# Two small matmul blocks of a gated DeltaNet kernel placed 22 matmuls behind their transpositions, one pacing rule for all pairs of heads, and a gate tile moved forward

## The chip, the cores and the metric

The kernel runs on one core of a Trainium2 chip. A core has a matrix engine, TensorE (PE in the profile; its weight loads have a row of their own, PEld), a vector engine (VectorE, DVE), a scalar engine for activations and copies (ScalarE, ACT), a general engine (GpSimd, POOL) and SyncE (SP), which here starts the large loads. The engines run side by side and wait for each other through semaphores. The metric is the time on the device in microseconds: 2536.32 us is the median of three runs of the kernel before (2536.3, 2536.32 and 2543.08). The profile comes from a further, separate execution.

## The reference

One layer of a streaming encoder over 512 positions of width 2048. All of it is in float32. Its parts:

```
proj = rmsnorm(x, g_pre) @ w_in                 # 145 column tiles of 128
q, k, v = silu(causal_conv4(qkv))               # 16 heads of 128
A = (k*beta) @ k.T * decay * strict             # per chunk of 64 positions
T = triangular_solve(I + A, I)                  # unit lower triangular
for chunk in 8: v_new, o, S = delta rule with T, decay and the running state S
o_a = rmsnorm(o, g_dn_out) * silu(z_a);  y_a = o_a @ w_br_a
u = silu(layernorm(causal_conv31(glu) + b_dw)) * silu(z_b);  y_b = u @ w_br_b
mixed = (sigmoid(gate_a)*y_a + sigmoid(gate_b)*y_b) @ w_out
x = x + rmsnorm(mixed, g_post)
x = x + rmsnorm(sigmoid(x @ w_ple_gate) * (p @ w_ple_proj), g_ple)
```

The change touches the third and fourth lines, where each pair of heads inverts its triangular blocks, and the place of one of the 16 tiles of gate_a.

## The kernel before

**The tile stream.** All large products run through `gemm_cm` (L169): a tile is one column block of 128 outputs by 512 positions, and takes 16 steps of the inner dimension. Every float32 operand is split in a high and a low part, so a step is three matmuls of 128x512 (L182, L184, L186; `g` is the accumulator): 48 for a tile. Jobs are queued in `jobs`, and `run_jobs` (L158) runs them in order. The weights come by SyncE into `raw`, are rounded by ScalarE (L127, the high part of `w`), and VectorE takes the rest (L128, the low part). When a tile is done, `evac` reads its accumulator. For a tile of q, k or v that is `conv4` (L405): one ScalarE operation (L408) and three VectorE operations (L410) on `cv`. For a gate tile it is one sigmoid on ScalarE (L716). There are two accumulators, so a tile's accumulator must be read before the next tile but one starts.

**What runs beside the stream.** The work for a pair of heads is a Python generator, `group(g)`, g from 0 to 7, spawned after the six q, k and v tiles of its pair. `tick()` (L142) is called after each of the 48 matmuls of a tile: it counts down every spawned generator and lets it emit its next instructions when its count is out. `yield n` asks for n matmuls of the stream before the next instructions, and a bare `yield` for HP = 4. So a number behind a yield is a distance on TensorE's queue, measured in matmuls of the stream. The layer that records the program keeps this order nearly as it is, and moves an instruction by a few places where its own estimate says that its input comes late. TensorE executes its matmuls in order: one whose input isn't there holds all behind it.

**Inside a group.** After transpositions and a 64x64 product for each chunk, VectorE inverts the 32x32 blocks by back substitution: 31 steps, each a product (L604, into `prod`) and a sum (L605, into `VT`). After each step the generator yields in proportion to the step's size times `pace`, 2.6 for the groups 0 to 6 and 1.85 for group 7 (L597). Then:

- VectorE transposes `VT` into `Vd` (L612); after one bare yield, for each of the four quadrants of 32 partitions, ScalarE copies `Vd` into `VP` (L618) and VectorE transposes that into `Tc` (L619).
- `yield 10`.
- TensorE computes `py` (L625, 16 products of 32x32; each reads the left half of `Tc`, which the quadrants 0 and 2 write) and `pz` (L628, 16 products of 64x64; each reads both halves of `Tc`). In the trace each float32 product of this kind is two matmuls, so 32 and 32.
- ScalarE copies `py` to `Y` (L632) and `pz` to `VP` (L635); 14 matmuls of the stream later TensorE computes `pd` (L640), from which ScalarE (L644) and VectorE (L646) complete `VP`.
- Ten matmuls later the scan over eight chunks starts, for both heads at once (`head_scan`, L446): in each chunk `psB` (L468), ScalarE's `vz` (L471), `psS` (L474), VectorE's new state `S` (L479), `psA` (L462), VectorE's `Xz` (L464), 14 matmuls of the stream for each chunk. It ends with `po` (L503, into the pool `wps` of two buffers), which VectorE reads (L511) into the head's output `oa`. The first product of the next group, `pk` (L532), takes a buffer of the same pool.

A group is spawned every eight tiles (six of q, k, v and two of z), so every 384 matmuls. Behind the last pair's two z tiles the queue holds three tiles of gate_a and the two tiles of the first GLU pair (L723 to L726). Then `finish("heads")` emits what is left of the last group without any stream beside it, and the buffers of the heads are given back. The next stage (L754 to L764) alternates tiles of `w_br_a`, the remaining gates and the GLU pairs, each of which spawns a convolution of 31 taps on VectorE.

Of the kernel before, what the change touches and what calls it, by code (L numbers as in the profile page):

```python
# [19 lines left out]
NK = D // P  # L20
NH = 16
# [61 lines left out]
def _body(ctx, tc, A, out):  # L83
# [82 lines left out]
    def w_in_tile(t):  # L166
        return A["w_in"][t]

    def gemm_cm(src, rhs, evac):  # L169
        if src is not None:  # L170
            prep_src.extend([src[0], src[1]])

        def job():
            ps = gps.tile([P, T], F32, tag="g", name="g")
            for qt in range(4):
                hi, lo = next_piece()
                for kk in range(4):
                    k = qt * 4 + kk
                    rh, rl = rhs[k]
                    wh = hi[:, kk * P:(kk + 1) * P]  # L180
                    wl = lo[:, kk * P:(kk + 1) * P]
                    mm(ps, wh, rh, start=(k == 0), stop=False)  # L182
                    tick()
                    mm(ps, wh, rl, start=False, stop=False)  # L184
                    tick()
                    mm(ps, wl, rh, start=False, stop=(k == NK - 1))  # L186
                    tick()
            evac(ps)
        jobs.append(job)
# [324 lines left out]
    def group(g):  # L514
# [79 lines left out]
        nc.vector.memset(UTf[:, 0:1024:33], 1.0)  # L594
        yield
        prod = hd.tile([P, 256], F32, tag="prod", name="prod", bufs=1)
        owed, pace = 0.0, 2.6 if g < NH // 2 - 1 else 1.85  # L597
        for j in range(30, -1, -1):
            n, i0 = 32 - j, j // 4
            ni = 8 - i0  # L600
# [10 lines left out]
        Vd = hd.tile([P, 8, 4, 8], F32, tag="Vd", name="Vd", bufs=1)  # L611
        nc.vector.transpose(Vd.rearrange("p i r x -> p (i r x)"), VT.rearrange("p j i -> p i j"))  # L612
        yield
        for qd in range(4):
            r = slice(32 * qd, 32 * qd + 32)
            b, par = 32 * (qd % 2), qd // 2
            dst = VP[r, :, par, b:b + 32]
            nc.scalar.copy(dst.rearrange("p x (i r) -> p x i r", r=4), Vd[r].rearrange("p i r x -> p x i r"))  # L618
            nc.vector.transpose(Tc[r, :, b:b + 32], dst)  # L619
        yield 10  # L620
        pz = wps.tile([P, 8, 64], F32, tag="w", name="pz")
        py = wps.tile([P, 8, 32], F32, tag="w", name="py")
        for x in range(8):
# [35 lines left out]
    for g in range(NH // 2):  # L659
        pair = (2 * g, 2 * g + 1)  # L660
        for h in pair:
            gemm_cm(w_in_tile(16 + h), hT, evac_k(h))
            gemm_cm(w_in_tile(h), hT, evac_q(h))
            gemm_cm(w_in_tile(32 + h), hT, evac_v(h))
        jobs.append(lambda g=g: spawn(group(g), HP, "heads"))
        for h in pair:
            gemm_cm(w_in_tile(Z_TILE0 + h), hT, evac_z(h))
# [38 lines left out]
    def glu_pair(i):  # L706
        gemm_cm(w_in_tile(GLU_TILE0 + 16 + i), hT, evac_glu_b(i))
        gemm_cm(w_in_tile(GLU_TILE0 + i), hT, evac_glu_a(i))
# [4 lines left out]
    def evac_gate(dst, i, col):  # L713
        def f(ps):
            gt = slots.tile([P, T], F32, tag="s", name="gt")
            nc.scalar.activation(gt, ps, AF.Sigmoid, bias=vv(V_BG + col))  # L716
            dst[i] = gt
        return f

    def gate_a(i):  # L720
        gemm_cm(w_in_tile(GATE_TILE0 + i), hT, evac_gate(mixed, i, i))

    for i in range(3):  # L723
        gate_a(i)
    glu_pair(0)
    run_jobs()  # L726
# [22 lines left out]
    def evac_ya(i):  # L749
        def f(ps):  # L750
            nc.vector.tensor_tensor(mixed[i], ps, mixed[i], ALU.mult)
        return f

    gate_a(3)  # L754
    glu_pair(1)
    jobs.append(lambda: finish("oa"))
    nglu = 2
    for i in range(NK):
        gemm_cm(A["w_br_a"][i], oT, evac_ya(i))
        if i + 4 < NK:  # L760
            gate_a(i + 4)
        if nglu < NK:
            glu_pair(nglu)
            nglu += 1  # L764
# [594 lines left out]
```

## Time and profile before

| | |
|---|---|
| median of three runs | 2536.32 us |
| the profiled execution, on the device | 2543.33 us |
| its span in the profile | 2541.6 us |
| mean granted TensorE clock | 0.991 |
| VectorE busy | 1652.4 us (65%) |
| ScalarE busy | 1054.8 us (42%) |
| DMA, mean rate | 110 GB/s |

The span is the time from the first to the last recorded instruction; the device time is 1.7 us longer. Busy time is what an engine spent in instructions, and idle time in front of an instruction is put down to whatever the instruction waited for last. The profile models the end of a matmul, and consecutive ones overlap: a 128x512 matmul is listed with 0.39 us, while the starts of two in a row lie 0.23 us apart, and it is the distance of the starts that says how fast the stream goes. "Granted clock" is the share of TensorE's full clock that it was given in a stretch. A timeline lists the start in us, the duration in us, the engine, the source line, the operation, the written and read tiles and their sizes, how often, and in brackets the idle time before it and what ended it.

### The profile page before, as it was taken

The page shows a single profiled execution, that of the slowest core. Times are in us where ns is not written, and L with a number is a line of the kernel's source. Part 1 is how long each engine was busy: PE and PEld are TensorE (multiplying, and loading weights), DVE is VectorE, ACT ScalarE, POOL GpSimd, SP SyncE. Part 2 cuts the span into 40 slices and gives each one's busy share as a digit, 9 for nine tenths or more (in the row PEclk, how much of TensorE's full clock was granted, in tenths as well). Part 3 has the DMA queues.
Part 4 walks back from the last instruction along what each step waited for, and adds up shares of the span by engine and source line. Part 5 has one row for each costly group of instructions (what it writes and reads, how often), then busy time and mean ns, then how long its engine had stood idle before and what let it go on. Part 6 is the DMA issues. An engine that isn't in the chain of part 4 may idle for free.

```text
span 2541.6 us, 32595 instructions
## 1 busy us (share of the span) xinstructions
PE 2490.6 (98%) x12202; PEld 2052.7 (81%) x12202; DVE 1652.4 (65%) x3092; ACT 1054.8 (42%) x2083; POOL 135.6 (5%) x151
## 2 busy tenths in 40 slices
PE   9999999999999999999999999999999999999998
PEld 7878787887878878888888888887888888787787
DVE  6766767767676775977786868947423334776744
ACT  6655454555545455322222222235422223544532
POOL 0100000000000000000000000002000000010000
PEclk9999999999999999999999999999999999999999
DMA  6322222222222222333333332432333223676552
GB/s 256 121 87 71 84 71 84 80 75 88 71 84 71 83 75 67 108 102 102 104 100 104 104 108 96 141 129 94 98 100 99 92 100 100 179 217 217 191 174 75
DMA packets 85406, 279.45 MB, mean 110 GB/s; under 512 B 9472, under 2 KB 9728, under 8 KB 85248
## 3 DMA queue, kind: packets, MB, share of 16 engines
q1 hardware_dynamic: 81792, 266.89, 31.5%
q0 software_dynamic: 2304, 8.39, 1.9%
q10 hardware_dynamic: 1152, 2.10, 0.3%
q8 instruction: 95, 1.56, 0.2%
q14 instruction: 63, 0.52, 0.1%
HBM read 262.66 MB, written 14.68 MB: 109 GB/s over the span
## 4 chain that ended last, share of the span: by engine, by line
PE 83%; DVE 11%; issue 2%; DMA 2%; ACT 1%; POOL 0%; SPq 0%; DVEq 0%; POOLq 0%; ACTq 0%
PE g L184 22%; PE g L186 22%; PE g L182 22%; DVE prod L604 3%; DVE VT L605 2%; DVE w L128 2%; PE f L1213 2%; DMA raw<-in_w_out 2%; PE f L1214 2%; PE f L1212 2%; PE psB L468 1%; PE f L1057 1%; PE psS L474 1%; DVE cv L410 1%; PE psA L462 1%
## 5 line engine op out<-in xcount | busy, mean ns | idle before, releaser
L186 PE MATMUL g<-hh,w 128*128 128x512 f32 x2320 | 921.0, 397 | 1.6 <-DVE w L128 1.6
L184 PE MATMUL g<-hl,w 128*128 128x512 f32 x2320 | 919.1, 396 | 0.0
L182 PE MATMUL g<-hh,w 128*128 128x512 f32 x2320 | 913.0, 394 | 0.0
L128 DVE TENSOR_TENSOR w<-raw,w 128x512 fp32r<-128x512 f32 x780 | 551.9, 711 | 479.8 <-ACT w L127 477.2
L127 ACT CAST w<-raw 128x512 fp32r<-128x512 f32 x780 | 479.1, 619 | 917.3 <-PE g L186 802.3
L186 PEld LDWEIGHTS g<-hh,w 128*128 128x128 f32 x2320 | 438.5, 189 | 88.8 <-DVE w L128 4.7
L184 PEld LDWEIGHTS g<-hl,w 128*128 128x128 f32 x2320 | 438.1, 189 | 88.7 <-issue 1.6
L182 PEld LDWEIGHTS g<-hh,w 128*128 128x128 f32 x2320 | 438.4, 189 | 85.4 <-issue 0.2
L689 DVE SCALAR_TENSOR_TENSOR uc<-sg,vec,uc 128x483 f32<-128x483 f32 (+14 forms) x480 | 351.8, 734 | 14.0 <-ACT uc L686 4.0
L410 DVE SCALAR_TENSOR_TENSOR cv<-g,vec,cv 128x511 f32<-128x511 f32 x144 | 106.2, 738 | 29.8 <-ACT cv L408 29.5
L182 PE MATMUL g<-oh,w 128*128 128x512 f32 x256 | 99.6, 389 | 0.0
L184 PE MATMUL g<-ol,w 128*128 128x512 f32 x256 | 99.6, 389 | 0.0
L186 PE MATMUL g<-oh,w 128*128 128x512 f32 x256 | 99.6, 389 | 0.0
L182 PE MATMUL g<-uh,w 128*128 128x512 f32 x256 | 99.6, 389 | 0.0
L184 PE MATMUL g<-ul,w 128*128 128x512 f32 x256 | 99.6, 389 | 0.0
L186 PE MATMUL g<-uh,w 128*128 128x512 f32 x256 | 99.6, 389 | 0.0
L604 DVE TENSOR_TENSOR prod<-UT,VT 128x2 f32<-128x2 f32 (+30 forms) x248 | 87.2, 352 | 6.7
L1057 PE MATMUL f<-wsp,oph 128*128 128x512 f32 x192 | 76.5, 399 | 4.4 <-DVE wsp L1033 4.4
L1056 PE MATMUL f<-wsp,oph 128*128 128x512 f32 x192 | 75.0, 398 | 2.8 <-ACT wsp L1032 2.8
L1213 PE MATMUL f<-w,xh 128*128 128x512 f32 x192 | 75.0, 391 | 1.9 <-DVE w L128 1.9
L1058 PE MATMUL f<-wsp,opl 128*128 128x512 f32 x192 | 75.4, 393 | 0.0
L1212 PE MATMUL f<-w,xh 128*128 128x512 f32 x192 | 75.1, 392 | 0.0
(298 smaller groups left out, 2685.8 us busy)
## 6 DMA issues: line engine op xcount, KB each, us to landing
raw<-in_w_in SPq DMA_DIRECT2D x290, 512.0 KB, 3.3
raw<-in_w_ple_gate SPq DMA_DIRECT2D x40, 512.0 KB, 3.4
raw<-in_w_out SPq DMA_DIRECT2D x35, 512.0 KB, 5.1
raw<-in_w_br_a SPq DMA_DIRECT2D x32, 512.0 KB, 3.3
raw<-in_w_br_b SPq DMA_DIRECT2D x32, 512.0 KB, 3.3
t<-in_w_out POOLq DMA_DIRECT2D x16, 512.0 KB, 7.4
rw<-in_w_out SPq DMA_DIRECT2D x9, 512.0 KB, 4.4
x<-in_x SPq DMA_DIRECT2D x8, 512.0 KB, 9.4
```

Of the source, the lines that this page charges most:

```text
L127: nc.scalar.copy(hi, rq)
L128: nc.vector.tensor_tensor(lo, rq, hi.bitcast(F32), ALU.subtract)
L182: mm(ps, wh, rh, start=(k == 0), stop=False)
L184: mm(ps, wh, rl, start=False, stop=False)
L186: mm(ps, wl, rh, start=False, stop=(k == NK - 1))
L410: nc.vector.scalar_tensor_tensor(y[:, s:], ps[:, 0:T - s], vv(w0 + 3 - s), y[:, s:], ALU.mult, ALU.add)
L604: pin(nc.vector.tensor_tensor(pv_, um, vm, ALU.mult))
L689: nc.vector.scalar_tensor_tensor(y[:, s:], u[:, 0:T - s], vv(w0 + TAPS - 1 - s), y[:, s:], ALU.mult, ALU.add)
L1057: mm(ps, lh, wl[:, c], start=False, stop=False)
L1058: mm(ps, ll, wh[:, c], start=False, stop=kk == 7)
L1212: mm(ps[tt], lh, wh, start=k == 0, stop=False)
L1213: mm(ps[tt], lh, wl, start=False, stop=False)
```

## The change

Four edits. The back substitution of the last pair is paced like the others (2.6). The four quadrants are copied and transposed in the order 0, 2, 1, 3. The distance between the transpositions and `py` and `pz` is 22 matmuls of the stream where it was 10. Four tiles of gate_a stand in front of the first GLU pair where three stood, the next stage begins with gate tile 4, and its loop adds gate tile i + 5. The number of tiles and of every kind of instruction stays the same.

```
-        owed, pace = 0.0, 2.6 if g < NH // 2 - 1 else 1.85
+        owed, pace = 0.0, 2.6
...
-        for qd in range(4):
+        for qd in (0, 2, 1, 3):
             r = slice(32 * qd, 32 * qd + 32)
             b, par = 32 * (qd % 2), qd // 2
             dst = VP[r, :, par, b:b + 32]
             nc.scalar.copy(dst.rearrange("p x (i r) -> p x i r", r=4), Vd[r].rearrange("p i r x -> p x i r"))
             nc.vector.transpose(Tc[r, :, b:b + 32], dst)
-        yield 10
+        yield 22
         pz = wps.tile([P, 8, 64], F32, tag="w", name="pz")
         py = wps.tile([P, 8, 32], F32, tag="w", name="py")
...
-    for i in range(3):
+    for i in range(4):
         gate_a(i)
     glu_pair(0)
...
-    gate_a(3)
+    gate_a(4)
     glu_pair(1)
...
-        if i + 4 < NK:
-            gate_a(i + 4)
+        if i + 5 < NK:
+            gate_a(i + 5)
```

What this does to the order of the instructions shows at three places. Counted in matmuls of the stream from its first tile, `py` of the group 0 stood behind 554 of them and now stands behind 566; `pd` moves from 568 to 580, the first `psB` from 578 to 591, and `po` from 704 to 716, while `pk` of the group 1 stays at 724. The same holds for the groups 1 to 6, each 384 later. In the group 7 `py` moves from 3200 to 3254 and `po` from 3350 to 3404; the stage's last tile ends at 3360 before and at 3408 now.

The first place is VectorE's queue in the group 0, from the transpositions into `Tc` to the first state `S`. Before:

```order
L619 STREAM_TRANSPOSE Tc<-VP 32x8x32 x3
L128 TENSOR_TENSOR w<-raw,w 128x512 x3
L646 TENSOR_TENSOR VP<-VP,pd 32x8x32 x2
L410 SCALAR_TENSOR_TENSOR cv<-g,vec,cv 128x511
L128 TENSOR_TENSOR w<-raw,w 128x512
L410 SCALAR_TENSOR_TENSOR cv<-g,vec,cv 128x510
L477 COPY S<-psS 128x128
```

And now:

```order
L619 STREAM_TRANSPOSE Tc<-VP 32x8x32 x3
L128 TENSOR_TENSOR w<-raw,w 128x512 x3
L410 SCALAR_TENSOR_TENSOR cv<-g,vec,cv 128x511
L128 TENSOR_TENSOR w<-raw,w 128x512
L410 SCALAR_TENSOR_TENSOR cv<-g,vec,cv 128x510
L646 TENSOR_TENSOR VP<-VP,pd 32x8x32
L410 SCALAR_TENSOR_TENSOR cv<-g,vec,cv 128x509
L646 TENSOR_TENSOR VP<-VP,pd 32x8x32
L128 TENSOR_TENSOR w<-raw,w 128x512
L477 COPY S<-psS 128x128 x2
```

The two additions that complete `VP` (L646), on which the first `psB` waits, stood ahead of the three convolution operations of the tile that ends at matmul 576; now they stand among them, since `pd` comes four matmuls after that tile's end and not eight before it.

The second place is ScalarE's queue at the same point, from the copy of `pz` on. Before:

```order
L635 COPY VP<-pz 64x8x64 x2
L127 CAST w<-raw 128x512
L644 COPY VP<-pd 32x8x32 x2
L408 ACTIVATE cv<-g,vec 128x512
L127 CAST w<-raw 128x512
```

And now:

```order
L635 COPY VP<-pz 64x8x64 x2
L408 ACTIVATE cv<-g,vec 128x512
L127 CAST w<-raw 128x512
L644 COPY VP<-pd 32x8x32 x2
L127 CAST w<-raw 128x512
```

The copies of `pd` (L644) changed places with the convolution's first operation (L408).

The third place is TensorE's queue in the group 7, around its `py` and `pz`. Before:

```order
L184 MATMUL g<-hl,w 128x512
L625 MATMUL py<-Tc,W 32x32
L186 MATMUL g<-hh,w 128x512
L182 MATMUL g<-hh,w 128x512
L628 MATMUL pz<-W,Tc 64x64
L184 MATMUL g<-hl,w 128x512
L625 MATMUL py<-Tc,W 32x32 x15
L628 MATMUL pz<-W,Tc 64x64 x15
L186 MATMUL g<-hh,w 128x512
```

And now:

```order
L184 MATMUL g<-hl,w 128x512
L625 MATMUL py<-Tc,W 32x32 x16
L628 MATMUL pz<-W,Tc 64x64 x16
L186 MATMUL g<-hh,w 128x512
L182 MATMUL g<-hh,w 128x512
```

The two blocks, which the recording layer had spread over four matmuls of the stream, now stand in one piece, as they do in the other groups before and after.

## The prediction, as it was recorded before the changed kernel was run

> **What bounds the kernel now.** I read the engines' shares first, then TensorE's waits, then the clock by group of heads, then the timeline at the waits.
>
> ```profile
> PE 2490.6 (98%) x12202; PEld 2052.7 (81%) x12202; DVE 1652.4 (65%) x3092; ACT 1054.8 (42%) x2083; POOL 135.6 (5%) x151
> ```
>
> ```profile
> PE py L625 <- DVE Tc L619: 21.4, 15, 6.4
> ...
> PE f L1213 <- DVE w L128: 1.9, 1, 1.9
> ...
> PE pv L556 <- ACT junk L552: 0.3, 1, 0.3
> ```
>
> TensorE is busy for 98% of the span, so only its waits and its slow stretches can be won. The list of its waits (total us, times, longest) is led by `py`, 21.4 us in 15 waits, all for the transpositions into `Tc`; the longest, 6.4 us, stands alone. The last row ends the list: nothing in the scan costs TensorE a wait of note.
>
> The second loss is no wait. Stretches from one group's first `py` to the next one's, each 384 matmuls of the stream (groups 0 to 3, and 5), with TensorE's busy time, the granted clock, and the share and rate of DMA:
>
> ```profile
> 178.00:290.92 112.92, 110.75 (x635) 0.97 0.23 78
> 290.92:403.74 112.82, 110.64 (x635) 0.97 0.24 78
> 403.74:516.45 112.71, 110.53 (x635) 0.97 0.24 78
> 516.45:626.40 109.95, 107.77 (x636) 1.00 0.25 80
> 736.26:847.72 111.46, 109.29 (x635) 0.98 0.24 78
> ```
>
> The same work takes 109.95 us at full clock (row four) and up to 112.9 us where the clock fell. In steps of half a microsecond the first fall and its end, and the second fall, read:
>
> ```profile
> 179.00:179.50 0.50, 0.03 (x2) 1.00 1.01 410
> 179.50:180.00 0.50, 0.50 (x22) 0.57 0.07 25
> 186.00:186.50 0.50, 0.50 (x3) 0.60 0.00 0
> 186.50:187.00 0.50, 0.50 (x4) 1.00 0.00 0
> 292.00:292.50 0.50, 0.14 (x5) 0.71 0.63 254
> ```
>
> The clock halves at about 179.57 (0.57 is 0.07 us at full and 0.43 us at half clock), while TensorE waits for `py`, and returns at about 186.4. It falls again at about 292.21.
>
> **The change, part by part.** *Groups 0 to 6, the wait.* Group 3, undisturbed by the clock:
>
> ```profile
> 515.17 0.39 PE L184 MATMUL g<-hl,w 128*128 128x512 f32 x1
> 515.88 0.42 DVE L619 STREAM_TRANSPOSE Tc<-VP 32x256 f32<-32x256 f32 x1
> 516.45 0.22 PE L625 MATMUL py<-Tc,W 32*32 32x32 f32 x2 [0.88 <-DVE Tc L619]
> 516.96 1.37 DVE L619 STREAM_TRANSPOSE Tc<-VP 32x256 f32<-32x256 f32 x3
> 517.92 0.69 PE L625 MATMUL py<-Tc,W 32*32 32x32 f32 x30 [1.26 <-DVE Tc L619]
> 518.53 1.15 PE L628 MATMUL pz<-W,Tc 64*64 64x64 f32 x32
> 519.61 0.50 PE L186 MATMUL g<-hh,w 128*128 128x512 f32 x1
> 519.95 0.39 PE L182 MATMUL g<-hh,w 128*128 128x512 f32 x1
> 520.18 0.40 PE L184 MATMUL g<-hl,w 128*128 128x512 f32 x1
> ```
>
> From the stream's last matmul ahead of the blocks to the first behind them pass 519.61 - 515.17 = 4.44 us. Without a wait it would be one step of the stream (0.23, the distance of the last two rows), 32 `py` at the pace of the 30 (0.61 / 30 x 32 = 0.65) and `pz` to the next matmul (519.61 - 518.53 = 1.08): 1.96, say 2.05 with a switch. So 2.4 us are there to be won, and the question is whether 22 matmuls win them all. Twelve steps more of 0.228 move the start of `py` from 515.40 to 518.13. By the trace the quadrants are transposed from 515.88 and from 516.96 on, three in 1.37 us; in the new order 2 is second, so `py` has its input at about 517.4, 0.7 us early. `pz` would start 0.65 us later, at 518.78, and the last quadrant ends at 518.33: 0.45 us of slack. VectorE's queue ahead of the transpositions stays as it was, and TensorE doesn't wait in that stretch now, so they aren't later. **7 x 2.4 = 16.8 us.** The order of quadrants alone costs nothing, the same eight instructions being issued.
>
> *The clock.* Above 109.95 us lie 2.97, 2.87, 2.76 and 1.51 us: **10.1 us**. The low stretch shrinks from 4.4 to 2.0 us of small matmuls without a pause; in group 3 the small matmuls and even the pauses went by at full clock (its row reads 1.00), so a fall needs a longer low stretch than the small matmuls alone make, and I take all of this as gone. The two falls lie 292.21 - 179.57 = 112.64 us apart.
>
> [...]
>
> *Group 7.* Its timeline, and then VectorE's costliest groups of instructions from 914 us to the first transposition into `Tc`:
>
> ```profile
> 946.83 0.39 PE L184 MATMUL g<-hl,w 128*128 128x512 f32 x1
> 953.61 0.28 PE L625 MATMUL py<-Tc,W 32*32 32x32 f32 x2 [6.39 <-DVE Tc L619]
> 960.85 0.57 PE L182 MATMUL g<-hh,w 128*128 128x512 f32 x1
> 961.26 0.39 PE L184 MATMUL g<-hl,w 128*128 128x512 f32 x1
> ```
>
> ```profile
> L604 DVE TENSOR_TENSOR prod<-UT,VT 128x2 f32<-128x2 f32 (+30 forms) x31 | 10.8, 350 | 0.9
> L128 DVE TENSOR_TENSOR w<-raw,w 128x512 fp32r<-128x512 f32 x12 | 8.1, 680 | 0.9 <-ACT w L127 0.9
> L605 DVE TENSOR_REDUCE VT<-prod 128x1 f32<-128x2 f32 (+30 forms) x31 | 7.9, 254 | 0.9
> ```
>
> From 946.83 to 961.26, when the stream is at full pace again, pass 14.43 us with nine steps of the stream in them (one at 946.83, eight from 953.82 to 960.85) and the two blocks. At full clock that is 9 x 0.228 + 1.73 + 0.1 = 3.9 us: **10.5 us** to be won. The three rows of the second view, the costliest groups on VectorE, are its work there: 10.8 + 7.9 + 8.1 = 26.8 us. The yields of the 31 steps add up to 56.4 x pace: 104 matmuls or 23.8 us at 1.85, which VectorE can't keep, and 147 or 33.4 us at 2.6, where it has some 27 us to do. So `Tc` is early then. The group needs 54 matmuls more of the stream; the gate tile moved in front is 48 of them, and `po` at 3404 still lies ahead of 3408.
>
> *The moved gate tiles.* The same number of tiles, loads and sigmoids; each convolution up to the 13th starts one tile later, the last three where they were. Covered as long as VectorE keeps up there; if the 13th and 14th, now three tiles apart like those behind them, held up `w`, the nearest row is the longest wait for `w` in the list of waits, 1.9 us, once. I take nothing.
>
> *What comes later on.* `pd`, the scan and `po` now meet the tiles' convolutions 12 matmuls further on. Now, in group 0:
>
> ```profile
> 189.12 0.41 DVE L646 TENSOR_TENSOR VP<-VP,pd 32x256 f32<-32x256 f32 x1 [0.98 <-ACT VP L644]
> 189.97 0.42 DVE L646 TENSOR_TENSOR VP<-VP,pd 32x256 f32<-32x256 f32 x1 [0.43 <-ACT VP L644]
> 190.76 0.69 ACT L408 ACTIVATE cv<-g,vec 128x512 f32<-128x512 f32 x1 [0.83 <-PE g L186]
> 191.03 0.61 PE L468 MATMUL psB<-Xz,VP 128*128 128x128 f32 x4
> 191.49 0.75 DVE L410 SCALAR_TENSOR_TENSOR cv<-g,vec,cv 128x511 f32<-128x511 f32 x1 [1.10 <-ACT cv L408]
> 192.15 0.68 DVE L128 TENSOR_TENSOR w<-raw,w 128x512 fp32r<-128x512 f32 x1
> 192.75 0.74 DVE L410 SCALAR_TENSOR_TENSOR cv<-g,vec,cv 128x510 f32<-128x510 f32 x1
> 193.61 0.74 DVE L410 SCALAR_TENSOR_TENSOR cv<-g,vec,cv 128x509 f32<-128x509 f32 x1
> ```
>
> The tile ends at about 190.7. In the new order the second L646 follows the third L410: 0.8 (to the first) + 0.7 + 0.6 + 0.7 for the three, 0.4, 0.7, 0.4 = 4.3 us behind the tile's end, and the first `psB` waits on it. It comes 15 steps and `pd` behind the tile's end, and `pd` is 32 small matmuls, at the pace of `pz` 1.1 us: 15 x 0.228 + 1.1 = 4.5 us. That is level. Bounds: a gain is excluded, as there is no such wait to lose; the other end is the whole of the three L410, 2.2 us a group. I take 0.2 us, near the sum: **1.4 us lost** in seven groups. `pk` follows `po` at 8 matmuls where it was 20, and needs a buffer that VectorE reads `po` from: 8 x 0.228 = 1.8 us are left as cover, and what is lost if they don't do stands with the third rival.
>
> Sum: 16.8 + 10.1 + 10.5 - 1.4 = 36.0. The span goes from 2541.6 to 2505.6, and with the 1.7 us around it (2543.33 - 2541.6) the execution from 2543.3 to **2507 us**. The profiled execution lies 7.0 us above the median of 2536.32. If it had more clock falls than the runs at 2536.3, those vanish with the rest and 2507 stands; if the 7 us lie elsewhere, a run without them gives 2500. I stay with 2507 and let the range reach below 2500.
>
> **The rivals.** *The waits go, the clock falls stay* (small matmuls alone pull the clock down): 2507 + 10.1 = 2517. For it: the clock is down while `py` and `pz` run. Against it: group 3, where both ran at full clock.
>
> *The transpositions are later than 22 matmuls, so the change doesn't do what it says.* With 0.45 us of slack, one more cast between the quadrants (0.68) leaves 0.2 us a group; if half the present wait stayed, 7 x 1.2 = 8 us and some falls with it: 2515 to 2520. Against it: VectorE's queue in front of them is the same.
>
> *The scan's start waits.* With 1 us at each first `psB` or `pk`: 2507 + 7 = 2514.
>
> *Slower.* One mechanism: in each of seven groups the convolutions of three tiles stand in front of a VectorE step of the scan, and TensorE waits for all of them, 3 x 0.74 = 2.2 us: 21 x 2.2 = 46 us, so 2507 + 46 = 2553. It decides from 37 / 21 = 1.8 us a tile on. Against it: two of three such meetings are there now, and the list of waits has no row for them.
>
> **How the numbers follow.** Forecast 0.70 (2499 to 2512), clock falls stay 0.12, `Tc` still late 0.08, scan's start 0.08, slower 0.02. The range 2498 to 2518 takes in the forecast, its bound and most of the next three. A measurement of this kernel can tell about 0.3% (7.6 us) from no change; all cases but the last are faster by more than that: 0.97, 0.01, 0.02.
>
> **What would show it.** Right: no row for `py` behind `Tc` among TensorE's waits; 107.5 us (109.95 - 2.4) from one group's `py` to the next at clock 1.00. Wrong: a new row for `psB` behind `VP` or `Xz`, or `pk` behind `oa`, of over 5 us; a clock of 0.97 in a group without a wait; in the group 7, `py` still behind `Tc`.

## The result, and the profile after

The changed kernel takes 2505.05 us (median of four runs, 2504.54 to 2505.59), the kernel before 2536.44 us in the same comparison: a ratio of 0.987 with a 95% interval of 0.9853 to 0.9887. By these medians the gain is 31.4 us. The profiled execution took 2505.59 us with a span of 2503.8 us, 37.7 us less than the profiled one of before. Two runs of the kernel before in the comparisons further down, of 4175 and 8855 us, were disturbed and are left out of every figure.

TensorE's waits after (engine, line, tile, what ended the wait, us in total, times, the longest):

```profile
PE e_ps L214 <- ACT w L127: 6.2, 1, 6.2
PE f L1057 <- DVE wsp L1033: 5.9, 7, 2.1
...
PE f L1213 <- DVE w L128: 2.0, 1, 2.0
PE g L186 <- DVE w L128: 1.6, 2, 1.2
...
PE pv L556 <- ACT junk L552: 0.3, 1, 0.3
```

The row that led the list, `py` behind `Tc` with 21.4 us, is gone, and none has come in its place: no `psB`, `po` or `pk`. What is left are waits of the start and of the last stages, as before. The stretches from one group's first `py` to the next one's, groups 0 to 6 (time, TensorE's busy time, granted clock, share and rate of DMA):

```profile
180.01:287.54 107.53, 107.53 (x636) 1.00 0.24 81
287.54:395.03 107.49, 107.49 (x635) 1.00 0.24 82
395.03:502.60 107.57, 107.57 (x636) 1.00 0.24 82
502.60:610.14 107.54, 107.54 (x636) 1.00 0.23 81
610.14:717.68 107.54, 107.54 (x636) 1.00 0.24 82
717.68:825.21 107.53, 107.53 (x635) 1.00 0.24 81
825.21:932.77 107.56, 107.56 (x635) 1.00 0.23 79
```

All seven are alike within 0.1 us, at full clock and without a gap: busy time equals the stretch. Before, those of the groups 0 to 5 took 109.9 to 112.9 us. The timeline of group 0 after, from the transpositions to the first `psB`:

```profile
177.67 0.42 DVE L619 STREAM_TRANSPOSE Tc<-VP 32x256 f32<-32x256 f32 x1
178.75 1.38 DVE L619 STREAM_TRANSPOSE Tc<-VP 32x256 f32<-32x256 f32 x3
179.69 0.39 PE L184 MATMUL g<-hl,w 128*128 128x512 f32 x1
180.01 0.69 PE L625 MATMUL py<-Tc,W 32*32 32x32 f32 x32
180.63 1.15 PE L628 MATMUL pz<-W,Tc 64*64 64x64 f32 x32
181.71 0.50 PE L186 MATMUL g<-hh,w 128*128 128x512 f32 x1
...
186.95 0.40 DVE L646 TENSOR_TENSOR VP<-VP,pd 32x256 f32<-32x256 f32 x1
187.28 0.73 DVE L410 SCALAR_TENSOR_TENSOR cv<-g,vec,cv 128x509 f32<-128x509 f32 x1
188.04 0.42 DVE L646 TENSOR_TENSOR VP<-VP,pd 32x256 f32<-32x256 f32 x1
188.76 0.60 PE L468 MATMUL psB<-Xz,VP 128*128 128x128 f32 x4
```

From the stream's last matmul ahead of `py` to the first behind `pz` pass 181.71 - 179.69 = 2.02 us, where group 3 took 4.44 before. The last quadrant ends at 180.13, half a microsecond before `pz` starts. Further down, VectorE's second L646 ends at 188.46, and the first `psB` starts at 188.76 without having waited. The matmul of `mean_ps` (L779), long after the heads and behind everything that the change touches, starts at 1672.3 us; before, at 1709.5. Those 37.2 us are nearly the whole gain between the two profiles: what comes later adds half a microsecond.

### The profile page after: what moved, and what is told of

It reads as the page before. It is cut to its first block, busy times and chain, and to the rows that moved or that the text cites. A ratio compares the mean times of both kernels' runs of the same rounds, so it can differ in the third digit from the quotient of the medians.

```text
span 2503.8 us, 32581 instructions
## 1 busy us (share of the span) xinstructions
PE 2472.1 (99%) x12202; PEld 2037.6 (81%) x12202; DVE 1655.5 (66%) x3092; ACT 1053.2 (42%) x2083; POOL 133.6 (5%) x151
## 4 chain that ended last, share of the span: by engine, by line
PE 93%; DVE 3%; DMA 2%; issue 1%; ACT 0%; POOL 0%; SPq 0%; DVEq 0%; POOLq 0%; ACTq 0%
PE g L184 26%; PE g L186 25%; PE g L182 25%; PE f L1213 2%; PE f L1214 2%; PE f L1212 2%; DMA raw<-in_w_out 2%; PE psB L468 1%; PE psS L474 1%; PE psA L462 1%; PE f L1057 1%; PE f L1058 1%; PE f L1056 1%; DVE wsp L1033 1%; PE pg L569 1%
## 5 line engine op out<-in xcount | busy, mean ns | idle before, releaser
L689 DVE SCALAR_TENSOR_TENSOR uc<-sg,vec,uc 128x511 f32<-128x511 f32 (+14 forms) x480 | 351.6, 734 | 14.0 <-ACT uc L686 3.9
```

Source lines behind the costliest of these rows:

```text
L689: nc.vector.scalar_tensor_tensor(y[:, s:], u[:, 0:T - s], vv(w0 + TAPS - 1 - s), y[:, s:], ALU.mult, ALU.add)
```

## The experiments

All ratios are to the kernel before, run on the same chip in the same comparison. In these comparisons the kernel before ran 27 times, from 2535.3 to 2548.9 us, with a median of 2539.8. The changed kernel itself ran only in the comparison above, from 2504.5 to 2505.6 us, so a difference of medians to it is one between comparisons. Where it is small, the start of `mean_ps` in the profiles says more: the part behind it took 828.4 to 833.8 us in the eleven profiles, without any link to the edit, and all edits lie in front of it.

**The distance alone.** The kernel before with one edit, for the groups 0 to 6 only:

```
-        yield 10
+        yield 22 if g < NH // 2 - 1 else 10
```

> The kernel before with 22 matmuls ahead of py in the groups 0 to 6 alone; order of quadrants, pace of the group 7 and gate tiles as before. My theory (the waits and the clock falls of the seven groups go by the distance alone, 16.8 + 10.1 us of the profile's 2543.3): 2514 to 2518 us, no wait for Tc in the groups 0 to 6, every group at clock 1.00 and 107.5 us from py to py, and the wait of about 6.4 us with its clock fall left in the group 7. Rival, the order of the quadrants is needed too: a wait of 0.3 us or more for py in each of the seven groups, 2517 us and more. Rival, the clock falls come from the small matmuls: 2525 us or so, and a clock of 0.97 in some of the groups.

Measured: 2515.37 us, ratio 0.9899 (0.9882 to 0.9916). In its profile the stretches from `py` to `py` of a group like the others and of group 6, which ends at the late `py` of group 7, and TensorE's wait in group 7, read:

```profile
717.53:825.09 107.56, 107.56 (x635) 1.00 0.25 81
825.09:926.87 101.78, 95.42 (x581) 0.98 0.21 73
```

```profile
PE py L625 <- DVE Tc L619: 6.4, 1, 6.4
```

The six stretches that can be compared, of the groups 0 to 5, take 107.54 to 107.57 us at clock 1.00, as in the changed kernel, with the quadrants in their old order, and none of the seven groups waits for `Tc`. The wait of group 7 is left as it was, with its clock fall. The difference to the changed kernel, 2515.37 - 2505.05 = 10.3 us, is what the other edits bring together; by the starts of `mean_ps` (1682.4 and 1672.3) it is 10.1.

**The pace and the gate tile alone.** The changed kernel with `yield 10` and `for qd in range(4)`.

> The changed kernel with the distance of 10 and the old order of quadrants: of the change, only the pace of the group 7 and the moved gate tile are left. My theory: the seven groups wait 2.4 us each again (16.8 us) and some of them lose 1.5 to 3 us by a clock fall, the group 7 loses at most what the others do (it has fewer VectorE operations in front of Tc): 2505 + 17 to 19 + 3 to 10 = 2525 to 2534 us, 5 to 10 us faster than before. Rival, the pace and the gate tile are worth nothing without the distance: 2536 us.

Measured: 2528.53 us, ratio 0.9951 (0.9935 to 0.9967). Its waits for `Tc`, and its stretches of the groups 1 to 5:

```profile
PE py L625 <- DVE Tc L619: 15.1, 14, 1.3
```

```profile
290.90:400.74 109.84, 107.67 (x634) 1.00 0.24 80
400.74:512.22 111.48, 109.29 (x634) 0.98 0.24 79
512.22:625.04 112.82, 110.64 (x634) 0.97 0.23 78
625.04:737.80 112.76, 110.53 (x635) 0.97 0.23 78
737.80:847.69 109.89, 107.71 (x635) 1.00 0.24 80
```

Fourteen waits, two to a group, 15.1 us: seven groups wait as before. In the timeline of group 7 `py` follows the stream without a wait, even at a distance of 10:

```profile
956.33 0.39 PE L184 MATMUL g<-hl,w 128*128 128x512 f32 x1
956.65 0.69 PE L625 MATMUL py<-Tc,W 32*32 32x32 f32 x32
```

The slower pace brought its `Tc` in time without the longer distance. The clock fell in other groups than in the profile of before (there the groups 0, 1, 2 and 5, here 0, 2, 3 and 4), by the same two sizes, about 1.6 and 2.9 us above 109.9: the groups do the same work, and the two profiles differ in which of them are hit.

**The order of the quadrants.** The changed kernel with `for qd in range(4)`.

> The changed kernel with the quadrants in the order 0, 1, 2, 3. My theory, with 22 matmuls all four quadrants are there before py needs its two: 2505 us, the same within 0.5 us, no wait for Tc. Rival, the order carries part of the gain: py waits 0.3 us or more in each of seven groups, 2507 us and more.

Measured: 2504.82 us, ratio 0.986 (0.9842 to 0.9878), and no wait for `Tc`. The new order brings nothing at this distance.

**The gate tile not moved.** The changed kernel with the old places of the gate tiles:

```
-    for i in range(4):
+    for i in range(3):
         gate_a(i)
...
-    gate_a(4)
+    gate_a(3)
...
-        if i + 5 < NK:
-            gate_a(i + 5)
+        if i + 4 < NK:
+            gate_a(i + 4)
```

> The changed kernel with three gate tiles in front of the first GLU pair as before. The group 7 then ends behind the stage's last tile: its last psB stands at 3369 and its po at 3375 and 3384, with matmuls of the next stage's first tile between them. My theory, the tail of the scan (two steps of its chain, squares, power, scaling, po) finds too little of the stream beside it, and TensorE waits in it: 3 to 12 us slower than the changed kernel, 2508 to 2517 us, with new waits for psB, psA or po behind the heads' operations. Rival, the matmuls of the next tile cover it: 2505 to 2506 us, so that the moved tile is worth nothing.

Measured: 2507.9 us, ratio 0.9869 (0.9854 to 0.9885), 2.9 us more than the changed kernel, just below the lower end of what I had expected. Its waits have one new row, and the timeline of the end of group 7 shows its place:

```profile
PE po L503 <- DVE O L498: 1.4, 2, 0.9
```

```profile
972.76 0.68 PE L468 MATMUL psB<-Xz,VP 128*128 128x128 f32 x4
974.33 1.01 POOL L494 TENSOR_TENSOR ors<-ors,mhalf_c 128x4 f32<-128x4 f32 x1 [90.64 <-DVE ors L492]
975.37 0.87 DVE L498 TENSOR_SCALAR O<-O,ors 128x128 f32<-128x128 f32 x4 [1.18 <-POOL ors L494]
975.71 0.72 PE L503 MATMUL po<-cst,O 128*128 128x128 f32 x3 [0.89 <-DVE O L498]
```

The tail of the scan runs into the next stage, where the recording layer puts only six matmuls of the stream between the last `psB` and the first `po`; power and scaling on POOL and VectorE take longer, and TensorE waits. `mean_ps` starts at 1675.7 us, 3.4 us later than in the changed kernel. The waits of `po` explain 1.4 of them; the rest isn't taken apart.

**Shorter and longer distances.** The changed kernel with `yield 16`, 13, 20 and 34.

> The changed kernel with a distance of 16 in place of 22. My theory, by the timeline of group 3: TensorE comes to py 1.37 us earlier, at 516.76, the second quadrant that py needs is there at about 517.45 (a wait of 0.7 us), and pz waits 0.3 us more for the last: 1.0 us a group, none in the group 7, 7 us in all, 2512 us. The low stretch is then 3.0 us where it was 4.4 before and 2.0 in the changed kernel; at most one or two groups lose 1.5 to 3 us by a clock fall: 2512 to 2515 us. Rival, a short pause pulls the clock down as often as the long one: 2520 us or more. Rival, 16 are enough: 2505 us.

Measured: 2515.43 us, ratio 0.9905 (0.9888 to 0.9921), just above what I had expected. The timeline of group 3 with 16 (TensorE's part):

```profile
504.62 0.39 PE L184 MATMUL g<-hl,w 128*128 128x512 f32 x1
504.94 0.24 PE L625 MATMUL py<-Tc,W 32*32 32x32 f32 x2
505.60 0.69 PE L625 MATMUL py<-Tc,W 32*32 32x32 f32 x30 [0.41 <-DVE Tc L619]
506.21 1.46 PE L628 MATMUL pz<-W,Tc 64*64 64x64 f32 x32
507.60 0.50 PE L186 MATMUL g<-hh,w 128*128 128x512 f32 x1
```

The stretch is 507.60 - 504.62 = 2.98 us, 0.96 above the changed kernel's 2.02, as I had reckoned (1.0); a third of it is hidden in `pz`, whose 32 matmuls take 1.46 us in place of 1.15. The whole group is 1.3 us longer (108.87 against 107.54); part of the rest is that `po` now waits 0.2 us too. No clock fell in a group of the profiled execution, though the low stretch of 3.0 us was half as long again as in the changed kernel. Seven times 1.33 us are 9.3, so 2514.4 us; `mean_ps` agrees, starting at 1681.4 us, 9.1 us later than in the changed kernel, and the remaining 1.0 us lies behind it, in the part that varies from run to run.

> The changed kernel with a distance of 13. My theory: TensorE comes to py at 516.08, waits 1.35 us there and 0.3 us at pz, 1.65 us a group or 11.6 us in seven, 2517 us; the low stretch is 3.65 us, and some groups fall: 2517 to 2525 us. Rival, falls need the whole 4.4 us of before: 2517 us and clock 0.999.

Measured: 2522.78 us, ratio 0.994 (0.9925 to 0.9955). Stretches of the groups 2 and 3:

```profile
399.40:509.12 109.72, 108.43 (x635) 1.00 0.25 80
509.12:620.39 111.27, 109.93 (x634) 0.98 0.24 79
```

A group without a fall (109.72) takes 2.2 us more than in the changed kernel. At the two blocks it loses what I had expected: from the stream's last matmul ahead of them to the first behind them pass 3.6 us in place of 2.02, 1.6 us. The rest lies further on in the group, 0.3 us of it in waits of `po`. Falls of 1.6 us or so hit two of seven groups (0 and 3).

> The changed kernel with a distance of 20. My theory, by the slack of 0.45 us at pz (two matmuls of the stream): it just does, 2505 to 2506 us, no wait for Tc above 0.1 us a group. Rival, the slack is smaller than I counted: 0.2 to 0.45 us lost in each of seven groups, 2507 to 2508 us.

Measured: 2506.68 us, ratio 0.9867 (0.9846 to 0.9889). A group takes 107.76 us, 0.2 more than with 22, and no wait for `Tc` is listed. The time, 2506.68 us, lies between those of the theory and of the rival. The rows on both sides of the two blocks in group 3 show the place:

```profile
502.39 0.39 PE L186 MATMUL g<-hh,w 128*128 128x512 f32 x1
502.71 0.69 PE L625 MATMUL py<-Tc,W 32*32 32x32 f32 x32
503.34 1.21 PE L628 MATMUL pz<-W,Tc 64*64 64x64 f32 x32
504.48 0.50 PE L182 MATMUL g<-hh,w 128*128 128x512 f32 x1
```

The stretch is 504.48 - 502.39 = 2.09 us, 0.07 above the changed kernel's 2.02, so at the blocks twenty are almost enough. The other 0.15 us of a group come later in it, where the scan's products stand at slightly different places of the stream; I didn't take them apart.

> The changed kernel with a distance of 34, twelve more than needed. po of a group now stands behind the place where the next group's pk stood (728 against 724), and the recording layer has moved pk to 738; the group 7 ends at 3408 with the stage. My theory, the group has no room left in its 384 matmuls: the two groups share the two buffers of wps, and TensorE waits for them, 0.5 to 2 us a group, 2508 to 2520 us, with a new wait at po, pk or pq. Rival, the order that the layer found covers it: 2505 to 2506 us, and a longer distance costs nothing.

Measured: 2511.48 us, ratio 0.9884 (0.9857 to 0.991): too far costs as well. A group takes 108.22 us, 0.7 more than with 22. The waits that I had expected, 0.5 to 2 us a group, aren't there; the only new one that the profile names is small:

```profile
PE pq L549 <- DVE ke L537: 0.5, 3, 0.2
```

So the time came out in the range, and the mechanism that I gave for it isn't shown. The finer mixture of `po`, `pk` and `pq` with the stream may account for the rest; I didn't take it apart.

**Small matmuls without a pause.** The changed kernel with `py` and `pz` computed three times over, by a loop around both blocks:

```
+        for _ in range(3):
             for x in range(8):
                 for a in (0, 64):
                     mm(py[a + 32:a + 64, x, :], U[a:a + 32, x, 32:64], Tc[a:a + 32, x, 0:32], start=True, stop=True)
...
```

> The changed kernel with the products py and pz computed three times in a row, with the same results: 5.2 us of small matmuls in each group without a pause, longer than the whole low stretch of before. My theory, only a pause pulls the clock down: 2 x 1.73 us more in each of eight groups and nothing else, 27.7 us, 2533 us, 111.0 us from py to py and the same clock as the changed kernel. Rival, the small matmuls themselves count as idle for the clock: falls in nearly every group, in which they take twice their time, 2550 us or more and a mean clock of 0.98 or less.

Measured: 2533.99 us, ratio 0.9978 (0.9969 to 0.9987). Three groups:

```profile
292.04:403.01 110.97, 110.97 (x764) 1.00 0.25 79
403.01:513.97 110.96, 110.96 (x764) 1.00 0.25 79
513.97:624.97 111.00, 111.00 (x764) 1.00 0.25 79
```

5.1 us of small matmuls in a row in every group, and the clock stays at 1.00 in all of them. The rival, falls from the small matmuls themselves, is out.

## Why the prediction was right, point by point

- **The waits of the groups 0 to 6, 16.8 us.** From 109.95 to 107.54 us a group, 2.41 us, seven times 16.9. The distance alone does it (the first experiment). The slack of 0.45 us, two matmuls, was nearly exact at the blocks themselves: 20 cost up to 0.07 us there and 16 the 0.96 us of the timeline. The order of the quadrants brings nothing at 22.
- **The clock, 10.1 us.** All groups stand at 1.00 after, so the term came out. The reason given for it was only half right. The prediction asked for a low stretch longer than the small matmuls alone make, as if these belonged to it. But 5.1 us of small matmuls in a row, more than the whole low stretch of before (4.4 us), drew no fall, while the 3.6 us with a distance of 13 did. In these runs the falls go with the pause. Counted as what the low stretch takes above 2.02 us, it was 2.4 us with a distance of 10 (falls in four groups of seven, in each of two profiles), 1.6 us with 13 (two of seven) and 0.9 us with 16 (none of seven, in one profile). What decides between a fall and none isn't shown.
- **The 7.0 us between the profile of before and the median,** which I had left open, are probably clock falls too, but no trace of a run at 2536 us was kept. Of the 27 runs of the kernel before, those with a mean clock of 0.994 took 2535.3 to 2539.8 us, those with 0.991, as in the profile, 2540.2 to 2543.5, and the slowest, 2548.9 us, had 0.989. Half a percent of 2540 us in mean clock is 25 us at a granted clock of 0.50. In the profile of before a step of the stream took 0.43 us at 0.50 (184 to 186 us) and 0.23 us at 1.00, so nearly half of the 25 us is lost, some 12 us, an estimate; the fastest and the slowest lie 13.5 us apart. So the clock term depends on the execution that one starts from: of the 31.4 us between the medians about 4 are left for it (31.4 - 16.9 - 10.3, an estimate), and against the median of the 27 runs the whole gain is 34.8 us. The forecast of the time hardly depends on this, as the changed kernel has no falls in the heads.
- **Group 7, 10.5 us.** In the changed kernel the two blocks of group 7 take 2.02 us and the other eight matmuls of the stream 8 x 0.228, against 14.43 us before: 10.6 us. The difference between the distance alone and the whole change is 10.3 us. The pace brought it: its `Tc` is early even at a distance of 10. The moved gate tile is its cover at the stage's end, worth about 3 us of the 10.3 (2.9 by the medians, 3.4 by `mean_ps`).
- **The new collision at the first `psB`, 1.4 us lost.** This term was mis-sized: nothing is lost. I had VectorE and TensorE level at 4.3 and 4.5 us behind the tile's end and took 0.2 us a group for safety; the trace has the second L646 done 0.3 us before `psB` starts.
- **The moved gate tiles, nothing.** The gains of the heads add up to 16.9 + 10.1 + 10.6 = 37.6 us, and `mean_ps` starts 37.2 us earlier, so little was lost between the heads and `mean_ps`. Between 985 us and `mean_ps` TensorE's list of waits is empty in the changed kernel, as it is before.

The sum without the 1.4 us is 37.4, and the two profiled executions lie 37.7 us apart. That it fits so closely holds for these two; the part behind `mean_ps` alone varied by 5.4 us over the profiles.

## What to carry to other kernels

A matmul placed too early cost more here than its own wait. Behind `py` of the group 7 the whole stream stood for 6.4 us; and in the groups 0, 1, 2, 5 and 7 of before, not in 3, 4 and 6, the granted clock fell to 0.50 within the pause or up to 1.6 us behind it, for 3.4 to 10.2 us. So place such an instruction by the producer's measured lag and little further: two matmuls fewer than 22 cost 0.2 us a group here, twelve more 0.7. When work beside a stream is slowed down or moved back, look for what covers its end: the tile moved in front made up about 3 of the 10.3 us that it and the slower pace gave together.

## What the runs showed of the hardware

The clock fell at short waits. In the profile of before TensorE had two waits of 0.9 and 1.3 us in each of the groups 0 to 6, with two small matmuls between them, and the clock fell in four of the seven. With a distance of 22 these waits are gone, and all seven stretches read 1.00. With a distance of 16 a wait of 0.4 us and 0.3 us inside `pz` drew no fall in the profiled run, and 5.1 us of small matmuls without a pause drew none either.

The falls can be timed. In half microseconds, the last fall among the groups 0 to 6 of before and the one at the wait of group 7, each with its end:

```profile
739.00:739.50 0.50, 0.50 (x19) 0.86 0.18 33
742.50:743.00 0.50, 0.50 (x3) 0.73 0.08 33
950.50:951.00 0.50, 0.00 (x0) 0.98 0.85 336
961.00:961.50 0.50, 0.50 (x4) 0.78 0.00 0
```

Read as in the prediction, they go from 739.36 to 742.77 and from 950.98 to 961.22, 3.41 and 10.24 us, where the fall of the prediction took 6.83 (179.57 to 186.40): once, three times and twice 3.41. The starts of these two lie 211.62 us apart, 62 times a third of 10.24 us, and the 112.64 us of the prediction are 33 such thirds. That is one profile; that other executions keep to it isn't shown. The fall of 3.41 us made group 5 1.5 us longer, those of 6.83 made the groups 0 to 2 2.8 to 3.0 us longer. Why the same pause drew a fall in some groups and none in others isn't shown either.

The kernel before, which has these pauses, varied more from run to run: 2535.3 to 2548.9 us in 27 runs. The variants without a fall in their profiled groups lay within 1.1 to 5.3 us, in four to ten runs each; the widest of these, the small blocks computed three times (2531.6 to 2537.0), had no wait for `Tc` at all, so not all of the variation comes from these pauses.
